# One Trainium2 core, a hybrid decoder layer: the first expert pair's row gather with its operands exchanged

## The chip, the core and the metric

The kernel runs on one core of one Trainium2 chip. The metric is the device time of one execution in microseconds (us). The core has a matrix engine (TensorE, PE in the profile; its weight loads are listed apart as PEld), a vector engine (VectorE, DVE), an activation engine (ScalarE, ACT), GpSimd (POOL), and SyncE (SP), which here only issues DMAs. Sixteen DMA engines move data between HBM and the on-chip memory SBUF. TensorE writes its results to PSUM, eight banks of 128 x 512 float32. The profile gives the TensorE clock that was granted, as a share of full speed.

## What is computed

The reference is one decoder layer on 512 tokens of 1024 features. The first half mixes tokens with two groups of attention heads; the second half is a mixture of 32 experts, of which each token uses two:

```python
h   = x + token_mixer(rmsnorm(x, norm_mix), ...)           # (512, 1024)
hn  = rmsnorm(h, norm_ffn)
out = h + hierarchical_moe(hn, ...)

def hierarchical_moe(t):
    # choose 1 of 4 groups, then 2 of its 8 experts: combine[token, expert] holds two gates per token
    y = 0
    for e in range(32):
        g = silu(t @ w_gate[e]) * (t @ w_up[e])             # 1024 -> 512
        y = y + combine[:, e:e+1] * (g @ w_down[e])         # 512 -> 1024
```

Every expert has three float32 matrices of 2 MiB, so the expert weights alone are 192 MiB, each byte of which is read once.

## The kernel before

The kernel has three stages. From 0 to about 255 us it does the input projection and the attention of eight head pairs, with an order of work written out by hand in half steps (the table PRM, lines 27 to 50). From about 255 to 302 us it does the output projection, the routing and the first gather. Then it goes through the experts, two at a time, in 16 pairs.

**Output projection and routing.** The last part of the output projection is a list of units (line 566): each is one 128-token tile i and one half of the 1024 output columns. A unit is twelve matmuls (op_mm, line 438), then op_ev on VectorE (line 452), which adds the result to the residual hx, [128, 4, 1024] in SBUF. For a finished half tile, route_half (line 658) squares it on ScalarE, transposes it on TensorE and, when the tile is whole, stores it to the DRAM scratch h_scratch (line 678). route_logit (line 681) makes the 36 router logits; top2 (line 707), a generator of nine VectorE steps, picks the experts of a tile and leaves the choice in mb (line 727). ranks (line 753) counts on TensorE which place each token takes in its expert's list, code_of (line 759) combines the two on VectorE, and pick_a (line 766) compares the places with a row of numbers: for pair q it makes a one-hot matrix of [tokens of tile i] x [128 slots], 64 slots for each of the two experts. The loop at line 889 mixes all that with the last six units; lines 911 to 946, written out by hand, finish it.

**The first gather.** Pair 0 needs its 128 token rows transposed, features on partitions: XT[0], [128, 8, 128]. It is made on TensorE by x_first (line 825) without waiting for the DRAM scratch. For each of eight 128-feature slices k and each tile i, the slice of the token rows is the stationary operand and the one-hot is the moving operand of 128 columns, so the sum over tiles comes out transposed. To keep the precision each tile is held as a high and a low part: tiles 0 and 1 as float16 scaled by the row's norm (split_h, line 786, buffer ha), tiles 2 and 3 as float32r (raw_hi on ScalarE and raw_lo on VectorE, lines 796 to 806, buffer hr). That makes 64 matmuls of 128 columns. The sums of four slices lie in one PSUM bank (FT, line 920), which two matmuls by a zero matrix open (line 925). x_first_ev (line 833) scales the eight slices by the feature gains, alternately on VectorE and ScalarE. Pairs 1 to 15 go another way: rows_in (line 842) fetches the rows from h_scratch with an indirect DMA into xg, [128, 1024], and x_rows (line 848) transposes them, four 128 x 128 blocks at a time, and scales them in one VectorE instruction.

**The experts.** mm_in (line 967) multiplies XT by the gate or the up matrix: 8 slices times 2 experts, 512 columns each, the two experts side by side in the array. After the first and after the second four slices it issues two weight loads. mm_down (line 993) does the down matrix. Among the first pair's matmuls stand the counting of pairs 0 and 1 (pick_g, line 814) and the fetch of pair 1's rows.

**The weight loads and their buffers.** Each load moves 1 MiB. There are 22 buffers of 1 MiB, the list units (lines 874 and 875), used in a ring: load number n goes into buffer n mod 22 (line 607). All loads are issued on SP, in order; SP waits in front of a load until the buffer's former reader is done, and everything behind it waits as well. Loads 0, 1 and 3 to 8 are issued before the routing stage. early (line 863) issues number 2 and numbers 9 to 18, into buffers that the attention stage gives up: slot (the second half), slotmhl1, slotmhl0a, slotr0, slotr6, slotmhl0b, slotr7a and slotr7b. late (line 880), called after the gather at lines 945 and 946, issues numbers 19, 20 and 21: one into the room of ha ("slots") and two into the room "wr". That room held the raw attention weights up to the last split_wo (line 431) and then, from line 798 on, hr. Load 22 is the first that reuses a buffer, that of the first gate matrix: it can go once the first half of the first mm_in is through.

Of the kernel before, what the change touches and what calls it, by code (L numbers as in the profile page):

```python
# [10 lines left out]
F32 = mybir.dt.float32  # L11
F32R = mybir.dt.float32r
# [4 lines left out]
OP = mybir.AluOpType  # L17
# [22 lines left out]
    g=[5, 10, 7, 2],  # L40
    sh=[14, 13],
    warm=[1, 9, 16],
    xr=[2, 6],
    lw=[96, 109, 111, 111, 119, 116, 133, 137],
# [539 lines left out]
def moe(ctx, tc, A, out, G):  # L584
# [63 lines left out]
    xg = sl.tile([128, 1024], F32, name="xg")  # L648
    pool.memset(xg, 0.0)
    ha = sl.tile([128, 2, 2, 1024], FP16, name="ha", tag="slots")  # L650
# [112 lines left out]

    OH0 = [me.tile([128, 2, 128], d, name="oh0" + n) for d, n in ((FP16, "h"), (F32R, "r"))]

# [27 lines left out]

    HR = {}

    def raw_hi(i, cs=(0, 1)):
        if not HR:
            t = G["ex"].tile([128, 2, 2, 1024], F32R, name="hr", tag="wr")
            HR.update({j: t[:, j - 2] for j in (2, 3)})
        for c in cs:  # L800
            act.activation(HR[i][:, 0, 512 * c:512 * c + 512], hx[:, i, 512 * c:512 * c + 512], AF.Copy)

    def raw_lo(i, eng, cs=(0, 1)):
        for c in cs:
            n = slice(512 * c, 512 * c + 512)
            eng.tensor_sub(HR[i][:, 1, n], hx[:, i, n], HR[i][:, 0, n])

    def part(h, k):
        return h[:, 512 * (k // 4):512 * (k // 4) + 512].rearrange("p (c k) -> p k c", k=4)[:, k % 4]
# [14 lines left out]

    def x_first(ks, tiles):
        for k in ks:
            o = FT[k // 4][:, k % 4, :]
            for i in tiles:
                for c in range(2):
                    h = part(HR[i][:, c] if i > 1 else ha[:, c, i], k)  # L830
                    pe.matmul(o, h, OH0[i // 2][:, i % 2, :], start=False, stop=(k % 4 == 3 and i == 3 and c == 1))

    def x_first_ev():
        XT[0] = G["m2_"].tile([128, 8, 128], F32, name="xT")
        for k in range(8):
            x, t, g = XT[0][:, k, :], FT[k // 4][:, k % 4, :], colx[:, k:k + 1]
            if k % 2:
                act.activation(x, t, AF.Copy, scale=g)
            else:
                v.tensor_scalar(x, t, g, None, op0=OP.mult)  # L840

# [21 lines left out]
    def early():  # L863
        G["st_wp"].close()
        nonlocal units
        sp = ctx.enter_context(spool("sp", "right"))
        r0 = sp.tile([128, 4096], F32, name="slotr0")
        r6 = ctx.enter_context(spool("sl2", "left")).tile([128, 2048], F32, name="slotr6")
        r5 = G["ex"].tile([128, 4096], F32, name="slotmhl1", tag="mhl1")
        r4 = [G["ex"].tile([128, 2048], F32, name="slot" + n, tag=n) for n in ("mhl0a", "mhl0b")]  # L870
        G["m2_"] = ctx.enter_context(spool("m2", "right"))
        sp = ctx.enter_context(spool("sp2", "right"))
        r7 = [sp.tile([128, 2048], F32, name=f"slotr7{c}") for c in "ab"]
        units = [t[:, 2048 * h:2048 * h + 2048] for t in [G["slot_x"], G["X"]["xh"], G["X"]["xl"]] + lslots + [r5, r0] for h in range(2)]
        units = units[:2] + units[6:7] + units[2:6] + [G["X"]["qkb"], G["X"]["qks"]] + units[7:10] + r4[:1] + units[10:] + [r6] + r4[1:] + r7
        for n in [2] + list(range(9, NS - 3)):
            state["n"] = n
            load()
# [10 lines left out]
    for u in range(10, 16):  # L889
        y = pend.pop(0)  # L890
        op_ev(*y)
        mid = {1: [route_b] * len(due_b), 2: [lambda: route_u(*y[:2])]}
        if u == 14:
            mid[3] = [lambda: raw_hi(2, (0,)), lambda: raw_lo(2, v, (0,))]
        if u == 15:
            mid[3] = [lambda: ranks([0, 1]), route_b, lambda: raw_hi(2, (1,))]
        for i in range(2):
# [10 lines left out]
        for i in range(2):  # L908
            if u == PRM["sh"][i]:
                split_h(i, (0,))  # L910
    xr = PRM["xr"]
    y = pend.pop(0)
    early()
    code_of(0, 2)
    pick_a(0, 0, 2)
    raw_hi(3, (0,))
    raw_lo(2, v, (1,))
    run(gen[2:3], PRM["g"][3])
    op_ev(*y, cut=(0, 256, 512))
    FT = [x.tile([128, 4, 128], F32, name=n) for x, n in ((pj, "pjt"), (psS, "ps_s"))]  # L920
    run(gen[2:3])
    route_u(*y[:2])
    raw_hi(3, (1,))
    for t in FT:
        pe.matmul(t, zero, one.unsqueeze(1).to_broadcast([128, 4, 128]), start=True, stop=False)
    x_first(range(xr[0]), (0, 1))
    ranks([2])
    code_of(2, 3)
    pick_a(0, 2, 3)
    raw_lo(3, v, (0,))  # L930
    route_b()
    x_first(range(xr[0], 8), (0, 1))
    run(gen[3:])
    raw_lo(3, v, (1,))
    pool.tensor_copy(gr[:, :, 0:1], ms2[:, :, 3:4])
    pool.tensor_copy(gr[:, 2:4, 2:3], ms2[:, 2:4, 3:4])
    x_first(range(xr[1]), (2,))
    ranks([3])
    x_first(range(xr[1], 8), (2,))
    code_of(3, 4)  # L940
    pick_a(0, 3, 4)
    x_first(range(8), (3,))
    x_first_ev()
    pick_h()
    late(sl, "slots", 1)
    late(G["ex"], "wr", 2)
    def gates():
# [318 lines left out]
```

## Time and profile before

| What | Value |
|---|---|
| Median of 3 runs | 769.19 us (766.52 to 770.28) |
| The profiled execution's own time | 767.02 us |
| Its span in the trace | 765.2 us |
| PE busy | 730.3 us, 95% |
| PEld busy | 441.6 us, 58% |
| DVE busy | 385.1 us, 50% |
| ACT busy | 185.1 us, 24% |
| POOL busy | 137.1 us, 18% |
| Read from HBM | 236.61 MB, 315 GB/s over the span |

The span leaves out 1.8 us of the execution's time around it. A busy share is an average over stages that have different limits, and a busy PE is not a PE at its peak, since the ends of its pipelined matmuls are modelled. The page of the profile shows the span in 40 equal slices of 19.1 us; other views give the same for any window, the instructions in order of time (start, duration, engine, line, shape, and in brackets the idle time before and what ended it), the chain of waits that ended last, and the instructions of one line. In the lists of time, instructions of one line that follow each other are merged, with their count behind an x; a float32 matmul counts as two instructions.

### The profile page before, as it was taken

What the parts mean: (1) busy time and instruction counts of PE and PEld (TensorE: products, weight loads), DVE (VectorE), ACT (ScalarE), POOL (GpSimd) and SP (SyncE); (2) the same over time, 40 slices, a digit from 0 to 9 for tenths busy, and PEclk for the clock granted to TensorE, in tenths of its full rate; (3) what the DMA queues carried; (4) which work ended last, traced back from release to release, by engine and by line L of the source; (5) the groups of instructions that cost most, each with busy time, mean ns of one, the idle gap of its engine ahead of it and who ended that gap; (6) DMA issues with size and microseconds to landing.
All of it is one profiled execution on the core that took longest, in us unless ns stands there. A gap on an engine that the chain in (4) does not pass through costs nothing.

```text
span 765.2 us, 10600 instructions
## 1 busy us (share of the span) xinstructions
PE 730.3 (95%) x3960; PEld 441.6 (58%) x3960; DVE 385.1 (50%) x939; ACT 185.1 (24%) x411; POOL 137.1 (18%) x228
## 2 busy tenths in 40 slices
PE   8989999999999999999999999999999998989996
PEld 7968877788887887334434443443443453543444
DVE  5698977777777556225324333432532431522423
ACT  6544444445433452111101111101110110101101
POOL 2776762332330410101100000000000000000000
PEclk9999999999999998999999999999999999999998
DMA  8621121352637569999999999999999999999994
GB/s 312 210 84 42 42 91 42 111 179 81 235 136 320 220 256 349 394 419 419 419 420 419 418 420 419 419 421 417 419 421 417 417 421 419 420 421 419 420 359 153
DMA packets 51637, 237.63 MB, mean 311 GB/s; under 512 B 6068, under 2 KB 17716, under 8 KB 27520
## 3 DMA queue, kind: packets, MB, share of 16 engines
q1 hardware_dynamic: 48848, 230.88, 75.9%
q0 software_dynamic: 2160, 3.95, 1.4%
q10 hardware_dynamic: 576, 2.10, 0.7%
q8 instruction: 32, 0.52, 0.3%
q14 instruction: 21, 0.17, 0.1%
HBM read 236.61 MB, written 4.21 MB: 315 GB/s over the span
## 4 chain that ended last, share of the span: by engine, by line
PE 57%; DMA 21%; DVE 11%; issue 4%; POOL 3%; ACT 2%; SPq 1%; DVEq 0%; POOLq 0%; ACTq 0%
PE ps_s L971 20%; PE pjt L999 10%; DVE hx L1114 3%; PE pjt L225 3%; DMA slotwr<-in_w_up_dram 3%; DMA slotslots<-in_w_up_dram 3%; DMA slotxh<-in_w_gate_dram 3%; DMA slotr7a<-in_w_up_dram 3%; PE po L388 3%; DMA slotr<-in_w_down_dram 3%; DMA slotmhl<-in_w_down_dram 3%; PE pjt L227 2%; PE pjt L226 2%; DMA wr<-in_wq_dram 2%; PE pjt L447 2%
## 5 line engine op out<-in xcount | busy, mean ns | idle before, releaser
L982 DVE SCALAR_TENSOR_TENSOR sg<-ps_s,idf,sg 128x512 f32<-128x512 f32 x16 | 12.0, 751 | 184.9 <-PE ps_s L971 184.9
L845 POOL DMA_INDIRECT xg<-h_scratch,rix x15 | 15.4, 1027 | 367.8 <-DVE at L859 282.7
L1012 ACT ACTIVATE yh<-pjt,idf 128x512 fp32r<-128x512 f32 x30 | 20.6, 687 | 136.8 <-PE pm L1112 70.3
L971 PE MATMUL ps_s<-slotxl,xT 128*64 128x512 f32 x112 | 49.9, 594 | 0.0
L989 ACT ACTIVATE hTt<-pt 128x512 f32<-128x512 f32 x16 | 9.6, 597 | 157.1 <-PE pt L987 157.1
L971 PE MATMUL ps_s<-slotxh,xT 128*64 128x512 f32 x104 | 46.3, 595 | 0.0
L363 ACT ACTIVATE z<-z,sm 128x128 f32<-128x128 f32 (+3 forms) x64 | 35.5, 555 | 43.0 <-DVE sm L361 42.9
L250 POOL TENSOR_TENSOR ss<-ss,mhalf 128x4 f32<-128x4 f32 x32 | 34.8, 1088 | 59.2 <-DVE ss L249 55.8
L1013 DVE SCALAR_TENSOR_TENSOR yl<-pjt,idf,yh 128x512 fp32r<-128x512 f32 x30 | 22.4, 748 | 45.5 <-ACT yh L1012 45.5
L971 PE MATMUL ps_s<-slot,xT 128*64 128x512 f32 x96 | 43.6, 595 | 1.3 <-DMA slot<-in_w_up_dram 1.3
L1114 DVE TENSOR_TENSOR hx<-hx,po 128x512 f32<-128x512 f32 x30 | 20.6, 688 | 43.9 <-PE po L1113 43.5
L971 PE MATMUL ps_s<-slotr,xT 128*64 128x512 f32 x136 | 39.5, 595 | 0.0
L226 PE MATMUL pjt<-wsa,xh 128*128 128x384 f32 (+1 forms) x112 | 38.1, 340 | 0.8 <-DVE wsa L148 0.8
L1114 DVE TENSOR_TENSOR hx<-hx,pt 128x512 f32<-128x512 f32 x60 | 38.3, 680 | 0.0
L980 ACT ACTIVATE sg<-ps_s,idf 128x512 f32<-128x512 f32 x16 | 11.0, 687 | 96.7 <-PE ps_s L971 96.7
L225 PE MATMUL pjt<-wsa,xh 128*128 128x384 f32 (+1 forms) x80 | 28.9, 362 | 0.4 <-ACT wsa L147 0.4
L382 DVE COPY PT<-pt 128x128 f32<-128x128 f32 (+3 forms) x64 | 28.2, 482 | 2.0 <-PE pt L381 1.7
L227 PE MATMUL pjt<-wsa,xl 128*128 128x384 f32 (+1 forms) x80 | 26.9, 336 | 0.0
L381 PE MATMUL pt<-ident,z 128*128 128x128 f32 x160 | 23.5, 277 | 3.5 <-DVE PT L382 2.2
L355 PE MATMUL ps_s<-qks 64*128 64x128 f32 (+3 forms) x192 | 25.0, 350 | 1.9 <-DVE qks L289 1.4
L225 PE MATMUL pjt<-wsu,xh 128*128 128x384 f32 (+1 forms) x72 | 26.6, 369 | 0.0
L226 PE MATMUL pjt<-wsu,xh 128*128 128x384 f32 (+1 forms) x76 | 26.0, 343 | 0.5 <-DVE wsu L148 0.5
(424 smaller groups left out, 1851.6 us busy)
## 6 DMA issues: line engine op xcount, KB each, us to landing
slotr<-in_w_gate_dram SPq DMA_DIRECT2D x11, 1024.0 KB, 19.9
wr<-in_wq_dram SPq DMA_DIRECT2D x28, 384.0 KB, 3.8
slotxh<-in_w_gate_dram SPq DMA_DIRECT2D x8, 1024.0 KB, 15.4
slotmhl<-in_w_down_dram SPq DMA_DIRECT2D x8, 1024.0 KB, 16.6
slotx<-in_w_down_dram SPq DMA_DIRECT2D x8, 1024.0 KB, 19.8
slotxl<-in_w_up_dram SPq DMA_DIRECT2D x7, 1024.0 KB, 20.5
slotxl<-in_w_gate_dram SPq DMA_DIRECT2D x7, 1024.0 KB, 18.8
slotr<-in_w_down_dram SPq DMA_DIRECT2D x7, 1024.0 KB, 19.9
```

The costliest lines, as they stand in the source:

```text
L225: pe.matmul(ps[:, :n], xh[:, k, t], wh, start=(k == 0), stop=False)
L226: pe.matmul(ps[:, :n], xh[:, k, t], wl, start=False, stop=False)
L227: pe.matmul(ps[:, :n], xl[:, k, t], wh, start=False, stop=(k == 7))
L250: pool.tensor_tensor(ss[:, 4:8], ss[:, 0:4], mhalf[:, 0:4], op=OP.pow)
L355: pe.matmul(pss[h][:, :n], q[d, t], k[d, :n], start=(k is kh and q is qh), stop=(q is ql))
L363: act.activation(z[:, :n], z[:, :n], AF.Exp, bias=nm, scale=-1.0, accum_out=l)
L381: pe.transpose(t[:, j, :], z[:, 128 * j:128 * j + 128], ident)
L382: v.tensor_copy(PT[p][h][:, :i + 1, 128 * i:128 * i + 128], t[:, :i + 1, :])
L388: pe.matmul(o[64 * h:64 * h + 64, 128 * j:512], V[p][:, j, 64 * h:64 * h + 64], PT[p][h][:, j, 128 * j:512], start=(j == 0), stop=(j == 3))
L971: pe.matmul(p[64 * e:64 * e + 64, :], XT[q][:, k, 64 * e:64 * e + 64], rows(q, u, e, k), start=(k == 0), stop=(k == 7))
L999: pe.matmul(DN[q, n][64 * e:64 * e + 64, :], HT[q][:, k, 64 * e:64 * e + 64], rows(q, 2, e, k)[:, 512 * n:512 * n + 512], start=(k == 0), ...
L1114: v.tensor_add(hx[:, i, ns], hx[:, i, ns], p)
```

## The change

The first gather is turned round. For tile i the one-hot is now the stationary operand and the token rows are the moving operand, 512 columns at a time, so that the sum comes out as rows, [128 slots, 1024], in two PSUM banks. Tiles 0 and 1 are still taken as float16 high and low parts: 4 matmuls a tile. Tiles 2 and 3 are taken straight from hx in float32: 2 matmuls a tile. raw_hi, raw_lo and the buffer hr are gone, the one-hot of tiles 2 and 3 is float32 and no longer float32r, and the two opening matmuls by a zero matrix are gone, since the first matmul on each bank now opens it. x_first_ev copies the two banks into the row buffer xg, one on ScalarE and one on VectorE, and then calls x_rows for pair 0 as for the others: eight transposes and two VectorE multiplications.

As hr is gone, the room "wr" takes its two loads (the buffer r1, numbers 12 and 13 now) in early, behind those of slotmhl1 and ahead of slotmhl0a; late issues only number 21. The memset of xg is dropped. The splits of tile 0 come two units earlier (sh).

```diff
@@ -38,9 +38,8 @@
     wo=[[115, 118, 114, 115], [126, 131, 127, 135], [135, 141, 141, 144], [145, 145, 146, 145]],
     rv=[[4, 0, 0], [4, 0, 1], [4, 0, 2], [4, 0, 3], [5, 0, 0], [5, 0, 1], [5, 0, 2], [7, 0, 1]],
     g=[5, 10, 7, 2],
-    sh=[14, 13],
+    sh=[12, 13],
     warm=[1, 9, 16],
-    xr=[2, 6],
     lw=[96, 109, 111, 111, 119, 116, 133, 137],
     cut=[256, 512, 768, 896],
     lx=133,
@@ -646,7 +645,6 @@
 
     sl = ctx.enter_context(spool("sl", "left"))
     xg = sl.tile([128, 1024], F32, name="xg")
-    pool.memset(xg, 0.0)
     ha = sl.tile([128, 2, 2, 1024], FP16, name="ha", tag="slots")
     rbig = me.tile([128, 2], F32, name="rbig")
     hd = nc.dram_tensor("h_scratch", (512, 1024), F32).ap()
@@ -761,7 +759,7 @@
 
     OHB = {}
 
-    OH0 = [me.tile([128, 2, 128], d, name="oh0" + n) for d, n in ((FP16, "h"), (F32R, "r"))]
+    OH0 = [me.tile([128, 2, 128], d, name="oh0" + n) for d, n in ((FP16, "h"), (F32, "r"))]
 
     def pick_a(q, a=0, b=4):
         if q:
@@ -790,20 +788,6 @@
             act.activation(hi, h, AF.Copy, scale=rbig[:, i:i + 1])
         if 1 in parts:
             v.scalar_tensor_tensor(lo, h, rbig[:, i:i + 1], hi, op0=OP.mult, op1=OP.subtract)
-
-    HR = {}
-
-    def raw_hi(i, cs=(0, 1)):
-        if not HR:
-            t = G["ex"].tile([128, 2, 2, 1024], F32R, name="hr", tag="wr")
-            HR.update({j: t[:, j - 2] for j in (2, 3)})
-        for c in cs:
-            act.activation(HR[i][:, 0, 512 * c:512 * c + 512], hx[:, i, 512 * c:512 * c + 512], AF.Copy)
-
-    def raw_lo(i, eng, cs=(0, 1)):
-        for c in cs:
-            n = slice(512 * c, 512 * c + 512)
-            eng.tensor_sub(HR[i][:, 1, n], hx[:, i, n], HR[i][:, 0, n])
 
     def part(h, k):
         return h[:, 512 * (k // 4):512 * (k // 4) + 512].rearrange("p (c k) -> p k c", k=4)[:, k % 4]
@@ -822,22 +806,19 @@
         v.tensor_copy(ID[q], p[:, 0:3])
         v.tensor_copy(ID[q][64:128, 2:3], p[64:128, 3:4])
 
-    def x_first(ks, tiles):
-        for k in ks:
-            o = FT[k // 4][:, k % 4, :]
-            for i in tiles:
-                for c in range(2):
-                    h = part(HR[i][:, c] if i > 1 else ha[:, c, i], k)
-                    pe.matmul(o, h, OH0[i // 2][:, i % 2, :], start=False, stop=(k % 4 == 3 and i == 3 and c == 1))
+    def x_first(tiles, gs=(0, 1)):
+        for i in tiles:
+            for g in gs:
+                n = slice(512 * g, 512 * g + 512)
+                for h in [ha[:, c, i, n] for c in range(2)] if i < 2 else [hx[:, i, n]]:
+                    pe.matmul(FT[g], OH0[i // 2][:, i % 2, :], h, start=not begun[g], stop=(i == 3))
+                    begun[g] = True
 
     def x_first_ev():
-        XT[0] = G["m2_"].tile([128, 8, 128], F32, name="xT")
-        for k in range(8):
-            x, t, g = XT[0][:, k, :], FT[k // 4][:, k % 4, :], colx[:, k:k + 1]
-            if k % 2:
-                act.activation(x, t, AF.Copy, scale=g)
-            else:
-                v.tensor_scalar(x, t, g, None, op0=OP.mult)
+        act.activation(xg[:, :512], FT[0], AF.Copy)
+        v.tensor_copy(xg[:, 512:], FT[1])
+        for g in range(2):
+            x_rows(0, g)
 
     def rows_in(q):
         ix = me.tile([128, 1], I32, name="rix")
@@ -866,14 +847,14 @@
         sp = ctx.enter_context(spool("sp", "right"))
         r0 = sp.tile([128, 4096], F32, name="slotr0")
         r6 = ctx.enter_context(spool("sl2", "left")).tile([128, 2048], F32, name="slotr6")
-        r5 = G["ex"].tile([128, 4096], F32, name="slotmhl1", tag="mhl1")
+        r5, r1 = (G["ex"].tile([128, 4096], F32, name="slot" + n, tag=n) for n in ("mhl1", "wr"))
         r4 = [G["ex"].tile([128, 2048], F32, name="slot" + n, tag=n) for n in ("mhl0a", "mhl0b")]
         G["m2_"] = ctx.enter_context(spool("m2", "right"))
         sp = ctx.enter_context(spool("sp2", "right"))
         r7 = [sp.tile([128, 2048], F32, name=f"slotr7{c}") for c in "ab"]
-        units = [t[:, 2048 * h:2048 * h + 2048] for t in [G["slot_x"], G["X"]["xh"], G["X"]["xl"]] + lslots + [r5, r0] for h in range(2)]
-        units = units[:2] + units[6:7] + units[2:6] + [G["X"]["qkb"], G["X"]["qks"]] + units[7:10] + r4[:1] + units[10:] + [r6] + r4[1:] + r7
-        for n in [2] + list(range(9, NS - 3)):
+        units = [t[:, 2048 * h:2048 * h + 2048] for t in [G["slot_x"], G["X"]["xh"], G["X"]["xl"]] + lslots + [r5, r1, r0] for h in range(2)]
+        units = units[:2] + units[6:7] + units[2:6] + [G["X"]["qkb"], G["X"]["qks"]] + units[7:12] + r4[:1] + units[12:] + [r6] + r4[1:] + r7
+        for n in [2] + list(range(9, NS - 1)):
             state["n"] = n
             load()
 
@@ -890,10 +871,8 @@
         y = pend.pop(0)
         op_ev(*y)
         mid = {1: [route_b] * len(due_b), 2: [lambda: route_u(*y[:2])]}
-        if u == 14:
-            mid[3] = [lambda: raw_hi(2, (0,)), lambda: raw_lo(2, v, (0,))]
         if u == 15:
-            mid[3] = [lambda: ranks([0, 1]), route_b, lambda: raw_hi(2, (1,))]
+            mid[3] = [lambda: ranks([0, 1]), route_b]
         for i in range(2):
             if u == PRM["sh"][i] + 1:
                 split_h(i, (1,))
@@ -908,42 +887,33 @@
         for i in range(2):
             if u == PRM["sh"][i]:
                 split_h(i, (0,))
-    xr = PRM["xr"]
     y = pend.pop(0)
     early()
     code_of(0, 2)
     pick_a(0, 0, 2)
-    raw_hi(3, (0,))
-    raw_lo(2, v, (1,))
     run(gen[2:3], PRM["g"][3])
     op_ev(*y, cut=(0, 256, 512))
-    FT = [x.tile([128, 4, 128], F32, name=n) for x, n in ((pj, "pjt"), (psS, "ps_s"))]
+    FT = [x.tile([128, 512], F32, name=n) for x, n in ((pj, "pjt"), (psS, "ps_s"))]
+    begun = [False, False]
     run(gen[2:3])
     route_u(*y[:2])
-    raw_hi(3, (1,))
-    for t in FT:
-        pe.matmul(t, zero, one.unsqueeze(1).to_broadcast([128, 4, 128]), start=True, stop=False)
-    x_first(range(xr[0]), (0, 1))
+    x_first((0,))
     ranks([2])
     code_of(2, 3)
     pick_a(0, 2, 3)
-    raw_lo(3, v, (0,))
     route_b()
-    x_first(range(xr[0], 8), (0, 1))
+    x_first((1,))
     run(gen[3:])
-    raw_lo(3, v, (1,))
     pool.tensor_copy(gr[:, :, 0:1], ms2[:, :, 3:4])
     pool.tensor_copy(gr[:, 2:4, 2:3], ms2[:, 2:4, 3:4])
-    x_first(range(xr[1]), (2,))
+    x_first((2,))
     ranks([3])
-    x_first(range(xr[1], 8), (2,))
     code_of(3, 4)
     pick_a(0, 3, 4)
-    x_first(range(8), (3,))
+    x_first((3,))
     x_first_ev()
     pick_h()
     late(sl, "slots", 1)
-    late(G["ex"], "wr", 2)
     def gates():
         sg_, e12 = tmp("sg_", 4, 1), tmp("e12", 4, 1)
         z = zm[:, :, :32]
```

## The prediction

> **What bounds the kernel now.** I read the page's 40 slices first: where the DMA stands still, and where the clock falls.
>
> ```profile
> PEclk9999999999999998999999999999999999999998
> DMA  8621121352637569999999999999999999999994
> GB/s 312 210 84 42 42 91 42 111 179 81 235 136 320 220 256 349 394 419 419 419 420 419 418 420 419 419 421 417 419 421 417 417 421 419 420 421 419 420 359 153
> ```
>
> PE is 95% busy, but from the 18th slice (325 us) the DMA moves 419 GB/s up to the last two. Windows set to the stages, then the chain of waits, say the same:
>
> ```profile
> 260.00:273.00 13.00, 12.92 (x78) 10.84 (x77) 4.20 (x13) 5.29 (x14) 3.01 (x11) 1.00 0.18 74
> 301.00:310.00 9.00, 9.00 (x54) 3.61 (x55) 4.11 (x19) 2.11 (x8) 0.00 (x0) 0.73 0.86 305
> 302.00:304.00 2.00, 2.00 (x6) 0.55 (x6) 0.96 (x5) 1.30 (x5) 0.00 (x0) 0.50 0.65 111
> 320.00:730.00 410.00, 397.93 (x1965) 175.81 (x1966) 147.77 (x277) 39.19 (x59) 17.32 (x29) 1.00 1.01 419
> 358.89 13.93 PE ps_s L971 x64
> 565.02 20.52 DMA slotr7a<-in_w_up_dram
> ```
>
> The last columns of a window are granted clock, DMA share and GB/s. From 320 to 730 us the share is 1.01 and the rate 419: the weight stream has no hole, and from 565 us the chain goes through its loads. So the stream sets the end, and since its bytes are fixed, time is won or lost only by holes in it. There are two near the change. From 260 to 273 us it moved 74 of 419 GB/s: 13 x (1 - 74/419) = 10.7 us empty. From 301 to 310 us it moved 305: 9 x (1 - 305/419) = 2.45 us empty. The issues on SP say what they wait for.
>
> ```profile
> 254.42 0.80 SPq L621 DMA_DIRECT2D slotmhl<-in_w_down_dram  x2
> 273.86 0.33 SPq L621 DMA_DIRECT2D slotmhl0a<-in_w_gate_dram  x1
> 294.14 0.33 SPq L621 DMA_DIRECT2D slotslots<-in_w_up_dram  x1
> 301.89 0.80 SPq L621 DMA_DIRECT2D slotwr<-in_w_down_dram  x2
> 307.49 0.80 SPq L621 DMA_DIRECT2D slotx<-in_w_down_dram  x2
> L435 DVE TENSOR_TENSOR wsa<-wr,wsa x6: 680/681/1157, 231.1 to 258.8; 128x512 fp32r<-128x512 f32 x6
> ```
>
> In the first hole SP stands before slotmhl0a, and the ring has nothing else to load. The two loads into "wr" go only at 301.89, after the last gather matmul, though that room's attention data was read for the last time at 258.8 + 0.7 = 259.5. Load 22 (slotx) goes at 307.49, when half of the first mm_in is through.
>
> **The early loads.** Numbers 12 and 13 go at about 259.5, behind slotmhl1 and 14 us before slotmhl0a, so that they hold up nobody. They are 2 x 1.049 MB / 419 GB/s = 5.0 us of transfer, in a hole of 10.7 us. At 301 us nothing is then left to load but number 22: from there the stream is empty until its data flow. A load into an empty queue takes a while: those of 301.89 left the two microseconds from 302 at 111 GB/s, 2 x (1 - 111/419) = 1.5 us, and 0.1 before 302. I take 1.6 us. So with R the issue of load 22, the gain is 5.0 + 2.45 - (R + 1.6 - 301) us, and nothing at R = 306.85. The rest is the search for R.
>
> **What leaves VectorE and PE ahead of it.**
>
> ```profile
> 281.84 0.69 DVE L806 TENSOR_TENSOR hr<-hx,hr 128x512 fp32r<-128x512 f32 x1 [1.39 <-ACT hr L801]
> 284.68 0.66 PE L668 MATMUL pt<-ident,hx 128*128 128x128 f32 x4 [0.35 <-DVE hx L456]
> 288.32 0.68 DVE L806 TENSOR_TENSOR hr<-hx,hr 128x512 fp32r<-128x512 f32 x1
> 289.25 0.87 DVE L456 SCALAR_TENSOR_TENSOR hx<-pjt,rg,hx 128x256 f32<-128x256 f32 x2
> 291.71 1.06 PE L684 MATMUL pm<-wrt,hT 128*128 128x36 f32 x8
> 293.29 0.26 DVE L690 SCALAR_TENSOR_TENSOR L<-pm,ms,L 128x36 f32<-128x36 f32 x1
> 295.44 0.19 DVE L727 TENSOR_TENSOR mb<-rt 128x32 bf16<-128x32 f32 x1
> ```
>
> The raw_lo at 288.32 stands in VectorE's queue right ahead of the last op_ev (289.25), from which tile 3's transposes, logits (291.71), top2 (from 293.55) and mb (done 295.63) follow one by one: 0.68 us. The one at 281.84 made VectorE wait 1.39 us for ScalarE and pushed the work behind it, so that PE stood 0.35 us before the transposes of 284.68; I take that as won. The shift is 1.03 us: logits done 291.74, mb done 294.60. The other two raw_lo, raw_hi, the memset and the splits' new place I cost at nothing: they lie in idle time of VectorE, ScalarE and POOL, while PE is busy with the projection. If that cover is gone it is at most the 1.3 us that one split_h takes on VectorE, so I let R vary by that.
>
> **The gather.**
>
> ```profile
> 290.45 0.38 PE L925 MATMUL pjt<-one,zero 128*128 128x512 bf16 x1
> 290.66 0.38 PE L925 MATMUL ps_s<-one,zero 128*128 128x512 bf16 x1
> 293.92 2.06 PE L831 MATMUL pjt<-oh0r,hr 128*128 128x128 f32 x8
> 296.85 0.18 PE L757 MATMUL po<-mb,slt 128*128 128x32 bf16 x1
> 297.29 0.29 DVE L770 TENSOR_TENSOR oh0r<-code,io 128x128 fp32r<-128x128 f32 x1
> 297.84 2.10 PE L831 MATMUL pjt<-oh0r,hr 128*128 128x128 f32 x8
> 299.74 2.12 PE L831 MATMUL ps_s<-oh0r,hr 128*128 128x128 f32 x8
> ```
>
> Before, mb was ready at 295.63 but the count (L757) came at 296.85, since 12 of tile 2's 16 matmuls stood ahead on PE at 0.26 us each; tile 3's 16 then ran to 301.86. After: a 16-bit matmul of 512 columns takes 0.21 us (290.45 to 290.66), so tile 1's four are 0.84. A float32 one takes 13.93 / 16 = 0.87 us: the 64 instructions of two mm_in are 32 matmuls, which run as 16 pairs side by side in the array's halves, and one of 128 columns fills both. No row here shows that form; the lower bound is a quarter of it (0.21), the upper one is the pair run one after the other (1.74), and I take 0.87, its own data type and length. PE: 291.74 + 0.84 + 2 x 0.87 = 294.3, before mb at 294.60, so that the count no longer waits for PE. Count at 294.65 to 294.83, then as in the rows (296.85 + 0.18 to 297.84) 0.81 us to the first matmul of tile 3: 295.64. Two of 0.87: 297.38, in place of 301.86.
>
> **From the sums to XT.**
>
> ```profile
> 290.71 0.60 ACT L676 ACTIVATE hT<-pt 128x512 f32<-128x512 f32 x1
> 299.98 0.35 DVE L840 TENSOR_SCALAR xT<-pjt,ks 128x128 f32<-128x128 f32 x1 [2.40 <-PE pjt L831]
> 301.79 5.67 PE L971 MATMUL ps_s<-slotx,xT 128*64 128x512 f32 x16
> 303.07 0.37 ACT L838 ACTIVATE xT<-ps_s,ks 128x128 f32<-128x128 f32 x1 [0.42 <-DVE xT L840]
> 320.30 0.72 PE L851 MATMUL po<-ident,xg 128*128 128x128 f32 x4 [1.32 <-DMA xg<-h_scratch,rix]
> 321.06 0.69 DVE L854 TENSOR_TENSOR xT<-po,ks 128x512 f32<-128x512 f32 x1 [1.31 <-PE po L851]
> ```
>
> The eight scalings (299.98 to 303.44) lay under the last matmuls, and mm_in began at once, at 301.79. Here the change loses: the second bank's copy on VectorE (0.69, as the row of the same size at 321.06) runs 297.45 to 298.15, the first bank's on ScalarE (0.60) is over by 297.2, four transposes (0.72) run 297.4 to 298.1, and the multiplication ends at 298.9. mm_in begins at 298.95; the second half's transposes and multiplication (to 299.7) hide under its first 16 instructions. Net on PE: 2.8 us sooner.
>
> **The clock.**
>
> ```profile
> 294.00:299.00 5.00, 5.00 (x27) 5.00 (x26) 2.48 (x11) 0.00 (x0) 0.00 (x0) 1.00 1.01 412
> 299.50:305.40 5.90, 5.90 (x20) 3.31 (x22) 2.73 (x13) 2.48 (x9) 0.00 (x0) 0.50 0.80 282
> ```
>
> mm_in's first 16 instructions took 5.67 us against 3.48 (a quarter of 13.93), as the granted clock was 0.50 from 299.5 to 305.4. It fell after 5 us in which PEld was busy throughout (294 to 299): short matmuls, each waiting for its float32r weights. That phase goes: after the change 0.84 + 1.74 + 1.74 us of the 5.6 us from 291.74 to 297.38 are 512-column streams. So I take the full clock: R = 298.95 + 3.48 + 0.03 = 302.45.
>
> [...]
>
> **The sum.** Empty after the change: 302.45 + 1.6 - 301 = 3.05 us. Gain: 5.0 + 2.45 - 3.05 = 4.4 us. The profiled execution, 767.02 us (span 765.2 and 1.8 around it), becomes 762.6; it lies 2.2 under the median of the runs shown, 769.19, which becomes 764.8. Two checks that the stream then stays full, from the issue rows
>
> ```profile
> 325.87 0.33 SPq L621 DMA_DIRECT2D slotqks<-in_w_up_dram  x1
> ```
>
> Loads 22 to 29 give it 20 us of work; load 30 came 18.4 us after load 22. In between lies the fetch of pair 1's rows, whose wait before (1.32 us at 320.30) stays, as it moves with load 22. And the counting ahead of it waits for VectorE's gate arithmetic, which begins at 299.7 in place of 302.9 and so keeps its distance to PE.
>
> **The rivals.** [...]
>
> *The early loads are not early* (the change doesn't do what it says: SP is held until about 274 by something other than the last read of "wr", and the 2 MiB reach 301 us as a remainder). Against: the row of L435. The 5.0 us are then not won, but the remainder fills the stream from 301 to 306, past R + 1.6 = 304.05, so that the second hole closes: gain 2.45 us, 766.7.
>
> *Slower: the low clock comes early and stays.* From 288 to 292 us PE has only short work; if the clock falls at 292.6, the four float32 matmuls double (1.74 each, which is also the upper bound of their price). Tile 2 ends at 296.1, the count and one-hot take 1.0, tile 3 ends at 300.6, XT is ready at 302.2, half of mm_in takes 6.96: R = 309.15, empty 9.75, 2.3 us slower: 771.5. It decides from R = 306.85 on. Against: the same gap at 288 to 290 did not lower the clock before 299.5.
>
> **How the numbers follow.** The forecast has 0.62, the clock at mm_in 0.23, late loads 0.08, slower 0.07. A measurement of this kernel can tell about 0.5%, 3.85 us, from no change. The forecast's 4.4 us has 1.3 us of unknown R and some 1.5 us of scatter of the medians (the runs shown spread over 3.8) around it, so about 0.7 of it lies beyond 3.85: 0.44 faster, and 0.01 from the two cases behind it. Slower by over 0.5% are 0.04, from the last case with a longer low clock. The range goes from 764.8 - 3.0 to the second case's 767.0 + 1.6.
>
> **What would show it.** Right: two slotwr issues near 259.5, and from 260 to 273 us about 235 GB/s in place of 74 (2.1 MB more in 13 us); tile 3's two float32 matmuls of 0.87 us; load 22 at 302 to 303 us; clock 1.00 at 299 to 305; 419 GB/s from 310. Wrong: slotx issued after 305, a float32 matmul far from 0.87 us, or a hole in the stream after 310 us, say before load 30, because the fetch of pair 1's rows did not move with load 22.

## The result, and the profile after

The changed kernel takes 760.73 us (median of 5 runs, 760.38 to 761.11); the kernel before, with two more runs beside it, 766.64 us (765.78 to 770.28). The ratio is 0.991, with a 95% interval of 0.9884 to 0.9936: 6.9 us faster, 4.9 to 8.9. The ratio goes by means; the medians differ by 5.9 us. A second measurement gave 760.03 us and 0.989 (0.9869 to 0.9911). The forecast was 764.8 us, in a range from 761.8 to 768.6: the direction was right, the measured time lies below the range.

The page of the changed kernel, its granted clock and its DMA in 40 slices:

```profile
span 758.8 us, 10505 instructions
...
PEclk9999999999999999999999999999999999999998
DMA  9621121352648859999999999999999999999995
GB/s 313 214 85 42 43 90 44 112 181 61 237 124 357 329 213 359 398 419 418 420 419 418 418 421 418 419 420 419 419 420 419 420 418 419 420 419 418 421 362 159
```

The 14th slice (246 to 265 us) went from 220 to 329 GB/s, and the stream is full from the 18th slice on, as before. The issues on SP, in order of time (start, duration, destination, count):

```profile
259.17 0.80 SPq L620 DMA_DIRECT2D slotwr<-in_w_gate_dram  x2
...
273.49 0.33 SPq L620 DMA_DIRECT2D slotmhl0a<-in_w_gate_dram  x1
...
294.14 0.33 SPq L620 DMA_DIRECT2D slotslots<-in_w_down_dram  x1
...
301.22 0.80 SPq L620 DMA_DIRECT2D slotx<-in_w_down_dram  x2
...
305.91 3.34 SPq L620 DMA_DIRECT2D slotxh<-in_w_gate_dram  x2
...
692.87 0.33 SPq L620 DMA_DIRECT2D slotxh<-in_w_down_dram  x1
```

The early loads went at 259.17 (forecast 259.5). Load 22, whose issue the prediction calls R, went at 301.22: 6.27 us earlier than before, where 5.04 were forecast. The row of 305.91 covers loads 25 and 26; its 3.34 us are the wait of load 26 for the next half of the matmuls. That gap isn't new: the kernel before has the same 3.34 us at 312.18. The last row is the load of a late pair; in the same view of the kernel before it stands at

```profile
698.96 0.33 SPq L621 DMA_DIRECT2D slotxh<-in_w_down_dram  x1
```

so 6.09 us of the 6.27 are still there 390 us later. The stream carried the gain to the end nearly one for one. The windows show out of which holes it came (last columns clock, DMA share, GB/s):

```profile
260.00:273.00 13.00, 12.92 (x77) 10.88 (x76) 4.02 (x12) 5.50 (x15) 1.74 (x8) 1.00 0.55 222
301.00:310.00 9.00, 9.00 (x64) 3.31 (x62) 2.07 (x8) 1.97 (x2) 1.30 (x1) 1.00 0.81 309
310.00:320.00 10.00, 8.04 (x48) 4.37 (x46) 3.25 (x8) 0.60 (x1) 0.96 (x1) 0.83 1.01 421
320.00:730.00 410.00, 399.79 (x1970) 173.97 (x1968) 147.95 (x276) 39.09 (x59) 16.37 (x29) 1.00 1.01 419
```

From 260 to 273 us: 222 in place of 74, 13 x 148 / 419 = 4.6 us of transfer won. From 301 to 310: 309 in place of 305, 0.1 us. From 310 to 320, where before it was 387: 10 x 34 / 419 = 0.8 us. With the 0.37 us by which this execution was already ahead at slotmhl0a (273.49 against 273.86), that is 5.9 of the 6.4 us between the spans. The prediction counted its second hole only up to 310 us, so the 0.8 us behind it stand in none of its terms.

The gather in the list of time of the changed kernel, from the router logits (L682) to mm_in (L941):

```profile
285.08 1.08 PE L682 MATMUL pm<-wrt,hT 128*128 128x36 f32 x8
...
287.29 0.87 DVE L455 SCALAR_TENSOR_TENSOR hx<-pjt,rg,hx 128x256 f32<-128x256 f32 x2
...
289.75 1.06 PE L682 MATMUL pm<-wrt,hT 128*128 128x36 f32 x8
...
290.85 0.26 DVE L688 SCALAR_TENSOR_TENSOR L<-pm,ms,L 128x36 f32<-128x36 f32 x1 [0.23 <-PE pm L682]
...
291.51 1.02 PE L814 MATMUL pjt<-hx,oh0r 128*128 128x512 f32 x2
...
292.37 1.02 PE L814 MATMUL ps_s<-hx,oh0r 128*128 128x512 f32 x2
...
293.00 0.19 DVE L725 TENSOR_TENSOR mb<-rt 128x32 bf16<-128x32 f32 x1
...
293.30 0.18 PE L755 MATMUL po<-mb,slt 128*128 128x32 bf16 x1
...
294.09 1.13 PE L814 MATMUL pjt<-hx,oh0r 128*128 128x512 f32 x2 [0.61 <-DVE oh0r L768]
...
295.06 1.02 PE L814 MATMUL ps_s<-hx,oh0r 128*128 128x512 f32 x2
295.26 0.60 ACT L818 ACTIVATE xg<-pjt 128x512 f32<-128x512 f32 x1 [5.92 <-PE pjt L814]
...
296.72 0.68 DVE L835 TENSOR_TENSOR xT<-po,ks 128x512 f32<-128x512 f32 x1
...
297.54 3.65 PE L941 MATMUL ps_s<-slotx,xT 128*64 128x512 f32 x16
```

A float32 matmul of 128 columns of weights and 512 of rows takes 0.86 us (291.51 to 292.37; 0.87 was taken). mm_in begins at 297.54 and its first 16 instructions take 3.65 us in place of 5.67, at a granted clock of 1.00 (297 to 305 us).

### The profile page after: what moved, and what is told of

The parts are those of the page before. It is cut to its first block, busy times and chain, and to the rows that moved or that the text cites. A ratio compares the mean times of both kernels' runs of the same rounds, so it can differ in the third digit from the quotient of the medians.

```text
span 758.8 us, 10505 instructions
## 1 busy us (share of the span) xinstructions
PE 726.5 (96%) x3918; PEld 435.9 (57%) x3918; DVE 383.8 (51%) x934; ACT 182.7 (24%) x404; POOL 136.1 (18%) x227
## 4 chain that ended last, share of the span: by engine, by line
PE 68%; DMA 13%; DVE 12%; issue 2%; ACT 2%; POOL 2%; SPq 0%; DVEq 0%; POOLq 0%; ACTq 0%
PE ps_s L941 22%; PE pjt L969 12%; DVE hx L1084 4%; PE pjt L224 3%; PE pjt L225 3%; PE pjt L226 3%; DMA slotslots<-in_w_up_dram 3%; DMA slotr7a<-in_w_up_dram 3%; PE po L387 3%; DMA slotwr<-in_w_down_dram 3%; DMA slotmhl<-in_w_down_dram 3%; PE pjt L446 2%; PE pjt L447 2%; PE pjt L448 2%; PE ps_s L354 2%
## 5 line engine op out<-in xcount | busy, mean ns | idle before, releaser
L941 PE MATMUL ps_s<-slotxl,xT 128*64 128x512 f32 x112 | 49.9, 595 | 0.0
L941 PE MATMUL ps_s<-slotxh,xT 128*64 128x512 f32 x104 | 46.3, 595 | 0.0
L941 PE MATMUL ps_s<-slot,xT 128*64 128x512 f32 x96 | 43.6, 595 | 1.3 <-DMA slot<-in_w_up_dram 1.3
L941 PE MATMUL ps_s<-slotr,xT 128*64 128x512 f32 x144 | 43.3, 595 | 0.0
```

The lines of the kernel that those rows point to most:

```text
L941: pe.matmul(p[64 * e:64 * e + 64, :], XT[q][:, k, 64 * e:64 * e + 64], rows(q, u, e, k), start=(k == 0), stop=(k == 7))
```

## The experiments

A caution for all of them: single executions differ, those of the changed kernel from 759.16 to 761.73 us, those of the kernel before by 4 to 7 us within one measurement, and the median of the kernel before was 766.64, 766.44, 766.80 and 765.80 us in the four measurements on which this section rests. The changed kernel itself was run in two of them only (760.73 and 760.03). So small differences between medians of different measurements tell little. R itself moves with the part of the run ahead of the change. Where a trace is compared, R is therefore counted from that execution's own issue of slotmhl0a, which lies ahead of the changed instructions: 33.63 us before, 27.73 us in the changed kernel.

**Early loads undone.** late takes the two loads again, behind the one into "slots"; the list of buffers goes back with it:

```diff
-        r5, r1 = (... for n in ("mhl1", "wr"))
+        r5 = G["ex"].tile([128, 4096], F32, name="slotmhl1", tag="mhl1")
...
     late(sl, "slots", 1)
+    late(G["ex"], "wr", 2)
```

> The changed kernel with one part undone: the two loads into the room wr go last again, after the one into slots (issued at about 294.5 us, no longer held by hr). The turned gather stays, so load 22 can be issued at R = 301.2 us as in the changed kernel. Theory A (the stream's restart: load 22's data flow at the later of R + 1.6 us and the moment at which the loads ahead of it are through): slots and wr are still moving until about 306 us, so load 22's data start 3.2 us later than in the changed kernel, 763.9 us. Rival B (the removed VectorE and TensorE work alone makes the gain): 760.7 us, no difference. Rival C (the 5.0 us of transfer moved into the early hole is the gain, whatever R): 765.7 us.

Measured: 761.66 us, ratio 0.9941 (0.9926 to 0.9956); the profiled execution 762.32 us, 1.7 more than the changed kernel's. R is the same 27.73 us: load 22 goes at 300.96. Its windows:

```profile
260.00:273.00 13.00, 12.92 (x77) 10.92 (x76) 4.02 (x12) 5.50 (x15) 1.48 (x6) 1.00 0.14 58
...
301.00:310.00 9.00, 9.00 (x64) 3.31 (x62) 1.80 (x7) 1.97 (x2) 1.30 (x1) 1.00 1.01 421
```

The first hole is open again (58 GB/s), and in exchange the second one is gone: the stream is full from 301 to 310 us. Theory A had the right sign and too large a size. Counted in the windows, 13 x 164 / 419 = 5.1 us are lost in the first hole, 9 x 112 / 419 = 2.4 won in the second and 0.9 between them (362 GB/s in place of 349 from 273 to 301 us): 1.8 us net. The expectation's 3.2 us are also what the prediction's formula gives, 5.0 won less 301.22 + 1.6 - 301 = 1.8 empty; it took the changed kernel's hole after 301 us as 1.8 us, where the window has 2.4, and had nothing between the holes. Rival C, 5 us, is out. Rival B, no difference, is out by the trace; by the medians alone (0.9 us, intervals that overlap) it would not be.

**R pushed back.** Six float32 matmuls that nobody reads, ahead of x_first_ev:

```diff
+    def stall(n):
+        t = psT.tile([128, 512], F32, name="pt")
+        for j in range(n):
+            pe.matmul(t, OH0[1][:, 1, :], hx[:, 3, 0:512], start=True, stop=True)
...
     x_first((3,))
+    stall(6)
     x_first_ev()
```

> The changed kernel with six float32 matmuls of 512 columns, whose result nobody reads, on TensorE between the gather and its transposes: 6 x 0.87 = 5.2 us, R = 306.4 us. Theory A: nothing else covers the time after 301 us, so the whole 5.2 us come out at the end, 765.9 us. Rival B: the same 765.9 us. Rival C: the early loads keep their gain, so at most 1 to 2 us slower, about 762 us.

The profiled execution took 1842.84 us, so its trace is not used; the median was 765.08 us, ratio 0.9983 (0.9969 to 0.9996). Once more, beside the changed kernel:

> The changed kernel with six float32 matmuls of 512 columns on TensorE between the gather and its transposes, once more, since the profiled execution of the first was disturbed. Their 5.2 us minus the 0.6 us that ScalarE's copy no longer adds put R at about 306 us. Theory A: no load is in flight after 301 us, so all of it comes out at the end: 4.5 to 5 us slower than the changed kernel, 765.5 us. Rival C (the 5.0 us of the early loads are the gain, whatever R): at most 2 us slower.

Measured: 764.36 us, ratio 0.9963 (0.9947 to 0.998), 4.3 us above the changed kernel of the same measurement (760.03), where theory A had 4.5 to 5 and Rival C at most 2. In the trace R is 306.69, 5.5 us later, and the time 766.43 against 760.61. The two holes in this execution:

```profile
260.00:273.00 13.00, 12.92 (x77) 10.86 (x77) 4.37 (x13) 5.13 (x14) 2.29 (x11) 1.00 0.63 243
...
301.00:310.00 9.00, 8.71 (x64) 3.86 (x64) 5.33 (x21) 0.58 (x3) 0.00 (x0) 1.00 0.35 117
```

**Both.** The stall, and the loads into "wr" last:

> The same stall, and the two loads into the room wr last. Theory A: the stream is busy with slots and wr until about 306 us and load 22 cannot go before 306 us either way, so the early loads are worth nothing here: within 0.5 us of the kernel with the stall alone. Rival C: 5 us slower than that. Together with the kernel whose wr loads are late without a stall, it shows that the early loads only pay as far as R comes before their end.

Measured: 765.51 us, ratio 0.9974 (0.9955 to 0.9994): 1.2 us over the stall alone, more than the 0.5 expected but inside the intervals; the two profiled executions took 766.43 and 766.54 us. The holes again:

```profile
260.00:273.00 13.00, 12.92 (x76) 10.79 (x75) 4.65 (x12) 4.76 (x13) 3.23 (x11) 1.00 0.27 111
...
301.00:310.00 9.00, 8.71 (x62) 3.88 (x62) 4.48 (x17) 0.59 (x3) 0.00 (x0) 1.00 0.84 330
```

What is lost in the first hole, 13 x 132 / 419 = 4.1 us, comes back in the second, 9 x 213 / 419 = 4.6. With R at 307 us the early loads are worth nothing that these runs can tell, nowhere near Rival C's 5 us. So the early loads pay only as far as R comes before the end of the late ones. The other half, that R pays in full only with nothing left to load, rests on the traces alone: counted from the issue of slotmhl0a, the stall costs 5.3 us with early loads and 2.5 with late ones, while the medians have 4.3 and 3.9.

**The splits put back, without use.** raw_hi and raw_lo at their old places, writing into xg, which is free until x_first_ev; tile 2's and 3's gather still reads hx:

```diff
+    def idle_hi(i, cs=(0, 1)): ...
+            act.activation(xg[:, n], hx[:, i, n], AF.Copy)
+    def idle_lo(i, cs=(0, 1)): ...
+            v.tensor_sub(xg[:, n], hx[:, i, n], xg[:, n])
```

> The changed kernel with the splits of tiles 2 and 3 put back at their old places and nothing read from them: four copies on ScalarE and four subtractions on VectorE, written into xg. The gather stays turned. Theory A with the prediction's sizes (0.68 us for the subtraction ahead of the last op_ev, 0.35 us for the stall of the transposes): R 1.0 us later, 761.7 us. Theory A with the sizes read from the changed kernel's trace (the chain to tile 3's choice was 2.1 us sooner, without the 0.37 us by which the whole run was ahead before the change): R 2.1 us later, 762.8 us. If the splits cost nothing, 760.7 us.

Measured: 762.90 us, ratio 0.996 (0.9942 to 0.9978), 2.2 us above the changed kernel's 760.73, near the 762.8 of the larger sizes. But R, 30.52 us after slotmhl0a, is 2.8 us later, and part of that is the clock: 0.53 from 288.0 to 291.6 us in this execution. The splits' own share is read from the point ahead of it: the last op_ev came 15.10 us after slotmhl0a, against 13.80 in the changed kernel and 15.39 before. That is 1.30 us.

**One subtraction at a time.** A VectorE subtraction that nobody reads, ahead of the last op_ev, and in another kernel ahead of tile 3's logits:

> The changed kernel with one VectorE subtraction of 128 x 512 (0.68 us, nobody reads its result) right ahead of the last op_ev, where a raw_lo stood. The prediction priced that place at its full 0.68 us: R 0.7 us later against the run's own issue of slotmhl0a (28.4 us after it, where the changed kernel had 27.73 in two executions), 0.6 us slower. If VectorE has idle time there, nothing.

> The changed kernel with the same subtraction ahead of tile 3's logits on VectorE, where another raw_lo stood. The prediction priced this place at nothing. What the two traces say: before, the logits' second instruction began 0.52 us after TensorE's last matmul, as the first had waited behind the raw_lo; after, 0.04 us. So R 0.3 to 0.5 us later against slotmhl0a; by the prediction 0.

The issues of slotmhl0a and of load 22 on SP, with the subtraction ahead of op_ev:

```profile
273.06 0.33 SPq L620 DMA_DIRECT2D slotmhl0a<-in_w_gate_dram  x1
...
301.39 0.80 SPq L620 DMA_DIRECT2D slotx<-in_w_down_dram  x2
```

and with it ahead of the logits:

```profile
274.01 0.33 SPq L620 DMA_DIRECT2D slotmhl0a<-in_w_gate_dram  x1
...
302.15 0.80 SPq L620 DMA_DIRECT2D slotx<-in_w_down_dram  x2
```

R is 28.33 and 28.14 us after slotmhl0a: 0.60 us later for the first place, 0.41 for the second, which the prediction had at nothing. The times, 761.67 (ratio 0.9941, 0.9918 to 0.9964) and 761.24 us (0.9935, 0.9909 to 0.996), cannot tell such small steps from each other; the traces can.

**Not turned.** The old orientation on float32 rows, and with it the two opening matmuls, the eight scalings and the memset of xg; early loads and no splits, as changed. The core of the edit:

```diff
-                for h in [ha[:, c, i, n] for c in range(2)] if i < 2 else [hx[:, i, n]]:
-                    pe.matmul(FT[g], OH0[i // 2][:, i % 2, :], h, start=not begun[g], stop=(i == 3))
+                for h in [part(ha[:, c, i], k) for c in range(2)] if i < 2 else [part(hx[:, i], k)]:
+                    pe.matmul(o, h, OH0[i // 2][:, i % 2, :], start=False, stop=(k % 4 == 3 and i == 3))
```

> The changed kernel with the gather in its old orientation, but with tiles 2 and 3 taken straight from hx in float32 as the stationary operand, 8 matmuls of 128 columns a tile, and the eight scalings in place of copies, transposes and multiplications. Early loads and no splits, as in the changed kernel. Theory A: tile 3's matmuls take 4 us (0.5 us each, two weight loads of float32 a matmul) in place of 1.9, the way from the last of them to mm_in is 1.5 us shorter, and the clock may fall again as weight loads bound PE (up to 2.2 us on mm_in): R 0.6 to 2.8 us later, 761.3 to 763.5 us. Rival B': the turning itself is the gain and the splits' removal and early loads bring nothing: about 766 us.

Measured: 764.28 us, ratio 0.9974 (0.9964 to 0.9984): 3.5 us over the changed kernel's 760.73 and 0.8 beyond the upper end of theory A; rival B', 766 us, is out. R is 31.11 us after slotmhl0a, 3.4 later, where at most 2.8 were expected. TensorE in order of time:

```profile
294.46 2.03 PE L815 MATMUL ps_s<-oh0r,hx 128*128 128x128 f32 x8
...
296.41 0.18 PE L756 MATMUL po<-mb,slt 128*128 128x32 bf16 x1
...
297.20 2.23 PE L815 MATMUL pjt<-oh0r,hx 128*128 128x128 f32 x8 [0.62 <-DVE oh0r L769]
299.23 2.07 PE L815 MATMUL ps_s<-oh0r,hx 128*128 128x128 f32 x8
```

The count stands behind tile 2's matmuls again (296.41 in place of 293.30), which the expectation left out, and tile 3 takes 4.1 us in place of 2.0. The clock fell again as well, to a mean of 0.79 from 297 to 305 us:

```profile
297.00:305.00 8.00, 7.80 (x34) 5.12 (x36) 3.04 (x14) 2.48 (x9) 0.00 (x0) 0.79 0.56 233
```

So the early loads and the missing splits are not enough: the turning is worth 3.4 of R's 5.9 us, the low clock included (1.00 from 297 to 305 us in the changed kernel).

**The changed kernel itself, beside the stall.**

> The changed kernel itself, beside the others of this call on the same chip. All theories: 760.7 us, about 0.991 of the kernel before.

The median was 760.03 us, but the profiled execution, 761.73 us, differs. Its issues on SP:

```profile
273.11 0.33 SPq L620 DMA_DIRECT2D slotmhl0a<-in_w_gate_dram  x1
...
303.84 0.80 SPq L620 DMA_DIRECT2D slotx<-in_w_down_dram  x2
```

and the window of the gather:

```profile
288.00:294.60 6.60, 6.60 (x23) 4.01 (x23) 3.79 (x21) 0.98 (x3) 1.37 (x5) 0.50 1.02 382
```

The granted clock was 0.50 over this window, and R came 30.73 us after slotmhl0a, 3.0 later than in the first profiled execution, where the same window shows

```profile
288.00:294.60 6.60, 5.82 (x32) 3.32 (x32) 4.62 (x25) 1.34 (x5) 1.37 (x5) 1.00 0.99 372
```

With the low clock PE is shown *busier* (6.60 against 5.82 us). The idle splits had such a fall too, to 0.53 from 288.0 to 291.6 us. Ahead of it PE had stood idle for 0.89 us here and 1.48 us there, before tile 3's transposes. But five other executions (the changed kernel's first, the unturned gather, the subtraction ahead of the logits, the stall, and the loads in halves below) stood there for 0.88 us and two, the kernel before and the one with the subtraction ahead of op_ev, for 1.49 us, all without a fall at 288 us. So the length of this idle time alone does not decide. To see whether the short idle times cause it at all, six bf16 matmuls that nobody reads were put into them (four ahead of tile 3's transposes, two ahead of its gather):

> The changed kernel with six bf16 matmuls of 512 columns, whose result nobody reads, where TensorE waits: four ahead of tile 3's transposes, two ahead of tile 3's gather. In one of two profiled executions of the changed kernel the granted clock was 0.50 from 288 to 294.6 us and load 22 went 3.0 us later against slotmhl0a, 1.1 us more in all. If the idle time there lets the clock fall, this kernel keeps 1.00 in every look, load 22 goes 27.7 us after slotmhl0a, and the median is 0 to 0.7 us below the changed kernel's 760.0 to 760.7, with less scatter. If the fall has another cause, it shows in some executions here too; the six matmuls alone cost nothing, or at most 0.4 us.

Measured: 760.20 us (759.08 to 761.41), ratio 0.9926 (0.9906 to 0.9947). The clock was 1.00 from 286 to 302 us in the profiled execution, with R at 27.73 us, so the six cost R nothing. But seven of the nine profiled executions with the turned gather and without them kept 1.00 from 273 to 301 us too (the other two have a mean of 0.88 and 0.94 there), and the scatter of the runs is no smaller. Whether the idle time causes the fall stays open.

**Loads cut in halves.** To bring R forward, the loads that pair 0's gate and up matmuls release were issued in two pieces of 512 KB each:

```diff
-            if k % 4 == 3:
+            if q == 0 and k % 2:
+                for c in range(2):
+                    load_half(state["n"] + c, k % 4 // 2)
+                if k % 4 == 3:
+                    state["n"] += 2
+            elif k % 4 == 3:
                 load()
                 load()
```

> The changed kernel with each load that pair 0's gate and up matmuls release cut in two of 512 KB: the first goes after two of the four slices, the second after all four. Theory A: the first halves of loads 22 and 23 go 1.7 us sooner, at 299.5 us, and their data flow from 301.1, just as the stream runs dry; the second hole (307 to 309 us) closes as well: 1.8 + 0.7 us faster than the changed kernel, 758.3 us. Rival D (the stream after 301 us is held by something else, say the fetch of pair 1's rows or SP's issue time): no difference, 760.7 us.

Measured: 760.00 us, ratio 0.9898 (0.9876 to 0.9919), no difference, although the first piece of load 22 went at 299.27 us. The window after 301 us, and the rate in 40 slices and the packets from 299 to 312 us:

```profile
301.00:310.00 9.00, 9.00 (x64) 3.31 (x62) 1.84 (x7) 1.97 (x2) 1.31 (x1) 1.00 0.96 327
```

```profile
GB/s 454 403 454 479 353 252 315 214 290 290 290 391 378 416 315 290 189 265 265 239 202 240 290 303 353 429 366 391 378 391 429 429 403 441 416 429 416 404 404 441
DMA packets 1211, 4.58 MB, mean 352 GB/s; under 512 B 203, under 2 KB 203, under 8 KB 1103
```

The DMA engines are busy 0.96 of the time, where the changed kernel has 0.81, yet the rate is 327 GB/s against 309. The row of the packets shows the difference: 900 packets of 2 to 8 KB; the changed kernel has 55 such (200 under 8 KB, 145 of them under 2 KB) from 301 to 314 us. The size of the packets is not the cause by itself, though, as the same execution shows further on:

```profile
310.00:320.00 10.00, 9.34 (x58) 4.09 (x56) 3.25 (x8) 0.60 (x1) 0.99 (x1) 1.00 1.03 412
```

The loads issued from 299.27 to 315.50 us are all such halves, and here the stream moves 412 GB/s. It is low from 302.9 to 306.2 us, about 280 GB/s as the mean of those slices, while the first halves are under way. Why they move so slowly there stays open. Theory A, in which R is all that counts, fails here: the halves bring the start forward and not the bytes. With only loads 22 and 23 cut, and the six matmuls kept:

> The kernel of the six extra matmuls, and in addition loads 22 and 23 (no others) cut in two halves of 512 KB, the first going after two of the four slices. Cutting all eight loads of pair 0's gate and up matmuls brought load 22 forward by 1.95 us and gained nothing: from 301 to 310 us the DMA share was 0.96 but only 327 GB/s, in pieces half as long. With only the two cut whose place is the dry time, the whole loads behind them should run at 380 GB/s and more: 0.5 to 1.2 us below the kernel with the six matmuls, 759 us or a little less. If halves cost as much as they bring here too, no difference.

Measured: 760.58 us (757.82 to 761.37), ratio 0.9926 (0.9903 to 0.9948). From 301 to 310 us the rate was 344 GB/s, not the 380 expected. The best single execution of all is among them, but the medians are the same. No version here beats the changed kernel by what a measurement can tell.

## Why the prediction was right or wrong

Two steps failed. The term for what leaves VectorE and PE ahead of the gather was taken at 1.03 us and measured 2.07. And the gain was taken from a base of 769.19 us, where five runs give 766.64. Of the 4.07 us between forecast and measurement 2.55 are the base; the rest is the gain between the medians, 5.9 us in place of 4.4.

**What bounds the kernel: right.** The end follows the weight stream. In nine profiled executions (the kernel before, the changed one twice, the stall, the unturned gather, the idle splits, the two single subtractions, the six matmuls) the time minus R lies between 457.9 and 460.5 us, while R goes from 301.1 to 307.5. The kernel before is among them: its late loads were through only at about 310 us (the slower one landed 8.1 us after its issue, at the latest 310.4), yet its stream still dipped to 295 GB/s from 308 to 309 us, so it was R that it waited for. Left out are the two kernels with late loads (461.4 and 458.9 us) and the two whose load 22 goes in halves. Within the 2.6 us of this spread R does not tell the time: the execution with the low clock came 2.6 us later in R than the first and 1.1 us later at the end.

**The early loads: right, but what stays empty behind them was too small.** They were issued at 259.17 and brought 4.6 us of transfer in the first hole against 5.0 worked out. With R at 301.22 the formula leaves 1.8 us empty after 301 us; the window from 301 to 310 us has 9 x 110 / 419 = 2.4. Undoing the loads alone cost 1.8 us net by the windows, where the formula has 3.2.

**What leaves VectorE and PE: the term that was too small.** The prediction had 1.03 us for the chain up to tile 3's choice. The traces, both counted from slotmhl0a, have 1.59 us up to the last op_ev and 0.48 more up to mb. Two things were missed. Ahead of the op_ev I took one PE stall of 0.35 us, the transposes of 284.68, where three stood in a row. The other two, in the list of time of the kernel before, with the logits behind them and with the VectorE rows for the second thing:

```profile
286.27 0.18 PE L757 MATMUL po<-mb,slt 128*128 128x32 bf16 x1 [0.16 <-DVE mb L727]
...
286.44 0.97 PEld L684 LDWEIGHTS pm<-wrt,hT 128*128 128x128 f32 x8 [0.41 <-ACT hT L676]
286.47 1.05 PE L684 MATMUL pm<-wrt,hT 128*128 128x36 f32 x8
...
292.33 0.68 DVE L806 TENSOR_TENSOR hr<-hx,hr 128x512 fp32r<-128x512 f32 x1
292.93 0.25 DVE L689 SCALAR_TENSOR_TENSOR L<-L,ms,ks 128x36 f32<-128x36 f32 x1
```

All three went: counted from slotmhl0a, the logits of 286.47 came 1.02 us sooner (285.08). And "The other two raw_lo ... I cost at nothing" was wrong for the one at 292.33: it held L689, and L690 waits behind that on the same engine. L690 began 0.52 us after PE's last matmul before, 0.04 after. The experiment with one subtraction there gives 0.41 us, the one ahead of the op_ev 0.60 against 0.68 priced. How the rest divides between the splits and the new place of split_h was not tried.

**The gather and the way to XT: right.** From mb's end to tile 3's first matmul 0.90 us (forecast 1.04), from there to mm_in 3.45 (3.31). The float32 matmul is 0.86 us.

**The clock at mm_in: right.** In the changed kernel the eight transposes (0.74 and 0.75 us for four) and a gap of 0.20 us stand there, the clock is 1.00, and the first 16 instructions take 3.65 us (3.48 forecast); in the execution whose clock had fallen earlier it is 3.67 from start to R. In all eleven profiled executions with the turned gather the clock is 1.00 under the first mm_in, and in the unturned one, where the short matmuls and their weight loads are back, it fell to a mean of 0.79 from 297 to 305 us: that supports the prediction's reason. The range's 767.0 us and the 0.23 for "the clock at mm_in" stand for a low clock behind the transposes; no run shows one there, and what the runs show in its place is 1.00.

**The slower rival happened in part.** The low clock did come early in one execution of the changed kernel, from 288 to about 294.6 us. It moved R by 3.0 us and ended 5.6 us ahead of the first mm_in, so it took a part of the gain and not all. That the first profiled execution was free of it is in part luck.

**The sum.** R came at 301.22 in place of 302.45: 0.37 us from the run's own start, 1.04 from the term above, -0.18 from the rest. With R as it came the formula gives 7.45 - 1.82 = 5.6 us in place of 4.4; the spans differ by 6.4.

**The number.** That alone would not have left the range. The other part is the base: 4.4 us were worked out against the profiled execution (767.02) and then taken from the median of three runs, 769.19. With five runs that median is 766.64, and three later sets of 24, 22 and 12 runs give 766.44, 766.80 and 765.80: the profiled execution was the better centre, and the three runs' spread of 3.8 us said that their median was not worth 2.2 us. From 766.64 the same working gives 762.2, and a range as wide would have held the measurement. The range should have been laid around both.

## What to carry to other kernels

When a stream of loads sets the end, count its holes in GB/s per window and ask of each edit which hole it closes; two edits that close the same hole don't add up, and one may be worth nothing without the other (here, behind the stall, the early loads won 4.1 us in one hole and lost 4.6 in the other). When an instruction is taken out of an engine's list of work, look at the first instruction behind it *and* at the one behind that (here L689 and L690, 0.41 us), and add up every stall in a row that the same lateness explains. And centre a forecast on the execution that the terms come from, not on a median of few runs.

## What the runs showed of the hardware

- Granted clock and a busy TensorE are different things. The same instructions ran at 1.00 in one execution and at 0.50 from 288 to 294.6 us in another, and PE is shown 100% busy in the second. An idle time of 0.88 or 0.89 us just ahead went before a fall in one execution of six.
- In the kernel before, eight float32r instructions of 128 columns, each with its own weights, took nearly the same time at both clocks: 1.90 us from start to start at 1.00 (from 293.92) and 2.05 us at 0.50 (from 299.74), about 0.25 us each. In the changed kernel four float32 instructions of 512 columns do tile 3 in 2.0 us (from 294.09), where sixteen float32 ones of 128 columns took 4.1 in the unturned gather (from 297.20).
- A high DMA share is not a high rate. Loads with 4 KB to a partition filled 0.96 of the DMA's time and moved 327 GB/s from 301 to 310 us, and moved 412 at 1.03 from 310 to 320 us; loads with 8 KB move 419 at 1.01 in the steady stretch.
- In the changed kernel TensorE waits 1.96 us for pair 1's rows, up to 314.68, and the clock falls: 0.51 from 314.7 to 317.9 us, 0.83 in the window from 310 to 320 us. The stream is at 421 GB/s there all the same.
